# A hand-written TensorE order through the compressed, selected-key and window attention of a hybrid transformer block

## The chip, the cores and the metric

One core of one Trainium2 chip. The metric is the device time of one execution in microseconds (us), the median of three runs. In the rows, PE is TensorE (matmuls; PEld its weight loads), DVE is VectorE, ACT is ScalarE, POOL is GpSimd, SP is SyncE, which issues the DMAs.

## What is computed

One block over 512 tokens of width 1024: a mixer of three attentions with gates, a memory attention, a SwiGLU feed-forward network, a last norm. All is fp32. The part around the change, cut from the reference:

```python
o_a = _stick_breaking(q_a, k_a, v_a)                 # branch 0
o_b = _dsa_attention(...)                            # branch 1
o_c = _nsa_attention(...)                            # branch 2
g = sigmoid(p['g_merge'])                            # u @ w_in, 3 x 1024 columns
merged = g[0]*(o_a @ w_up[0]) + g[1]*(o_b @ w_up[1]) + g[2]*(o_c @ w_up[2])
h = h + merged @ w_out
# _dsa_attention, per block of 128 queries, 4 heads:
score = einsum('bqh,bqhk->bqk', wi, relu(qi . k_idx)); causal mask
sel = top_k(score, 128)                              # min(256, 512 // 4)
o_b = softmax over the selected keys (one k and v for all heads)
# _nsa_attention, per block of 128 queries, 4 heads:
o_c = gb[0]*softmax(q . kc) @ vc                     # 31 compressed keys
    + gb[1]*causal softmax(q . k_sel) @ v_sel        # all 8 blocks of 64 are selected
    + gb[2]*window softmax(q . k_win) @ v_win        # window 512: all causal keys
```

## The kernel before

**Number format.** Each fp32 operand of the large products is split into a high and a low part, and each product is three matmuls (`mm3`, L94 to L96: high by high, high by low, low by high). The weight tiles come by DMA from SP through rings: `load_fill` (two tiles; high part cast on ACT at L58, low part subtracted on POOL at L66) and `load_split` (three tiles; low part on DVE, L66).

**Stages.** Norm and projections; the stick-breaking attention (branch 0); then the part of the change; then memory attention, `w_out`, feed-forward network, last norm. The 512 queries go in tiles i = 0 to 3 of 128; query tile i sees (i + 1) x 128 keys.

**C attention** (branch 2, lines 618 to 624). For each tile three units: compressed keys (`cmp_attention`), selected blocks and window (`rows_attention`, once each). A `rows_attention` unit has for each of four heads two score matmuls (L292, L293) into one of the two banks of the pool `gm`, a fused subtraction and minimum on DVE that empties the bank (L578) and an exponential on ACT (L579). Then come a reciprocal, four scalings (L586 on ACT), and for each 128 keys `apply_v`: four transposes (L565), a copy out of PSUM (L58 or L60), and two value matmuls (a `pair`, L101) that add into the bank `av`. `pr`, which holds the probabilities, has two buffers; `pt`, the transposed copy, three.

**Selected-key attention B** (branch 1). Its keys are chosen by 16 rounds for each of tiles 1 to 3 (`topk_rounds`): DVE searches the eight largest scores of each row (L615) and replaces them (L616), over 256, 384 or 512 columns. 96 instructions in all. Then a mask (L631) and four `rows_attention` units with scalings and copies on DVE (lines 633 to 637).

**Gates and merges.** `fill_gate(j, f)` is one gate, 128 columns of branch j: 24 matmuls of 128x512 into one of the two banks of the pool `gf`, then a tanh on ACT. There are eight for each branch; three for branch 0 stand earlier in the program. `merge_up` multiplies a branch by `w_up` (eight steps of six matmuls), takes the product with the gate on DVE and adds the branches on POOL. In the program all of these stand behind both attentions (lines 639 to 646).

**What sets the order.** The kernel is written through a framework whose scheduler orders each engine's instructions when the program is built: among those that its own cost model holds ready, the one that is earliest in the program goes first. So gate matmuls, latest in the program, fill in where it holds attention work not to be ready, and the top-k rounds, later in the program than C, fill DVE in the same way. On the chip every engine then takes its instructions strictly in that order, each waiting until its inputs and its buffer are there.

```python
    for i in range(NT):
        o_ps = av_ps.tile([P, 2, P], F32, name="av")
        cmp_attention(i, o_ps, True, False)
        rows_attention(i, qc, ksel, vs["vsel"], causal_bias(i), gates[:, i, 1::3], o_ps, False, False)
        rows_attention(i, qc, kwin, vs["vwin"], causal_bias(i), gates[:, i, 2::3], o_ps, False, True)
        split(o_c[0][:, :, cc(i)], o_c[1][:, :, cc(i)], o_ps, scale=0.5)
    for r in range(16):
        for x in range(1, NT):
            topk_rounds(x, 1)
```

Of the kernel before, what the change touches and what calls it, by code (L numbers as in the profile page):

```python
# [7 lines left out]
F32 = mybir.dt.float32  # L8
# [18 lines left out]
def block_kernel(ctx: ExitStack, tc: tile.TileContext, A, out, dbg=None):  # L27
# [337 lines left out]
    def merge_gate(j, f, g, load, bank, cols=slice(0, S)):  # L365

        w = load((NK, P), [col_view(w_in, 2128 + j * D + f * P, P)])
        for k in range(NK):
            mm3(bank, [t[:, k, :] for t in w], [t[:, k, cols] for t in uT], k == 0, k == NK - 1)
        if j == 0 and f < early_g:  # L370
            nc.scalar.copy(g, bank)
        else:
            nc.scalar.activation(g, bank, AF.Tanh, scale=0.5)

    def fill_gate(j, f, n=S):
        g_t[j, f] = gp_.tile([P, S], F32, name="g", bufs=16)
        gp = gf_ps.tile([P, 512], F32, name="gf")
        merge_gate(j, f, g_t[j, f][:, :n], load_split if j == 1 and f % 2 else load_fill, gp[:, :n], slice(0, n))
# [11 lines left out]
    def merge_up(j, name, load, up_ps, n=S):  # L390
        for f in range(NK):
            if f % 4 == 0:
                w = load_up(j, f // 4, load)
            g, first = g_t[j, f][:, :n], g_t[0, f][:, :n]
            if j == 0 and f < early_g:
                with tc.issue_after(last_exp[0]):
                    nc.scalar.activation(g, g, AF.Tanh, scale=0.5)
            up = up_ps.tile([P, 512], F32, name=up_tag[up_ps is gf_ps])
            add_up(w, f, name, g, up[:, :n], slice(0, n))
            if j == 1:  # L400
                nc.vector.tensor_add(first, first, g)
                split(mg[0][:, f, :n], mg[1][:, f, :n], first, lo_eng=nc.gpsimd)
            elif j == 2:
                nc.gpsimd.tensor_add(first, first, g)

    for f in range(early_g):
        fill_gate(0, f)
# [153 lines left out]
    def apply_v(o_ps, v, src, first, last, k=P, eng=nc.scalar):  # L561

        tp = ps.tile([P, 4, P], F32, name="ps")
        for h in range(4):
            nc.tensor.transpose(tp[0:k, h, :], src[:, h, :], ident)  # L565
        pt = mq.tile([P, 4, P], F32, name="pt", bufs=3)
        copy(eng, pt[0:k], tp[0:k])
        pair(o_ps, [v, v], [pt[0:k, x::2, :] for x in range(2)], first, last)

    def rows_attention(i, q, k, v, bias, gate, o_ps, first, last, eng=nc.scalar):  # L570
        n = (i + 1) * P
        pr = mq.tile([P, 4, 512], F32, name="pr", bufs=2)
        nm = mq.tile([P, 4], F32, name="nm", bufs=2)
        den = mq.tile([P, 4], F32, name="den", bufs=2)
        for h in range(4):
            st = gm_ps.tile([P, 512], F32, name="gm")
            scores(st[:, :n], q[:, h, cc(i)], [t[:, 0:n] for t in k])
            nc.vector.tensor_tensor_reduce(pr[:, h, :n], st[:, :n], bias, -1.0, 3e38, ALU.add, ALU.min, nm[:, h:h + 1])  # L578
            nc.scalar.activation(pr[:, h, :n], pr[:, h, :n], AF.Exp, bias=nm[:, h:h + 1], scale=-1.0, accum_out=den[:, h:h + 1])  # L579
        sc = mq.tile([P, 4], F32, name="sc", bufs=2)  # L580
        nc.vector.reciprocal(sc, den)
        if gate is not None:
            nc.vector.tensor_mul(sc, sc, gate)
        for h in range(4):
            if eng is nc.scalar:
                nc.scalar.activation(pr[:, h, :n], pr[:, h, :n], AF.Copy, scale=sc[:, h:h + 1])  # L586
            else:
                nc.vector.tensor_scalar(pr[:, h, :n], pr[:, h, :n], sc[:, h:h + 1], None, op0=ALU.mult)
        for j in range(i + 1):
            apply_v(o_ps, v[:, j, :], pr[:, :, cc(j)], first and j == 0, last and j == i, eng=eng)  # L590

    def cmp_attention(i, o_ps, first, last):
        s = mq.tile([P, 4, 32], F32, name="cs")
        st = ps.tile([P, 4, P], F32, name="ps")
        for h in range(4):
            scores(st[:, h, 0:32], qc[:, h, cc(i)], kc)
        nc.vector.tensor_add(s, st[:, :, 0:32], cmpb[:, i, :].unsqueeze(1).to_broadcast([P, 4, 32]))
        m = mq.tile([P, 4], F32, name="nm", bufs=2)
        nc.vector.tensor_reduce(m, s, axis=AX.X, op=ALU.max)
        nc.vector.tensor_scalar(m, m, -1e20, None, op0=ALU.max)  # L600
        nc.vector.tensor_sub(s, s, m.unsqueeze(2).to_broadcast([P, 4, 32]))
        nc.scalar.activation(s, s, AF.Exp)
        den = mq.tile([P, 4], F32, name="den", bufs=2)
        nc.vector.tensor_reduce(den, s, axis=AX.X, op=ALU.add)
        nc.vector.tensor_scalar(den, den, 1e-30, None, op0=ALU.max)
        sc = mq.tile([P, 4], F32, name="sc", bufs=2)
        nc.vector.reciprocal(sc, den)
        nc.vector.tensor_mul(sc, sc, gates[:, i, 0::3])
        nc.vector.tensor_mul(s, s, sc.unsqueeze(2).to_broadcast([P, 4, 32]))
        apply_v(o_ps, vc, s, first, last, k=32)  # L610
# [8 lines left out]
    for i in range(NT):  # L619
        o_ps = av_ps.tile([P, 2, P], F32, name="av")  # L620
        cmp_attention(i, o_ps, True, False)
        rows_attention(i, qc, ksel, vs["vsel"], causal_bias(i), gates[:, i, 1::3], o_ps, False, False)
        rows_attention(i, qc, kwin, vs["vwin"], causal_bias(i), gates[:, i, 2::3], o_ps, False, True)
        split(o_c[0][:, :, cc(i)], o_c[1][:, :, cc(i)], o_ps, scale=0.5)
    dump("o_c", o_c[0].bitcast(F32))
    for r in range(16):
        for x in range(1, NT):
            topk_rounds(x, 1)


    for i in range(1, NT):  # L631
        nc.vector.tensor_scalar(score[i], score[i], -2e38, NEG, op0=ALU.is_gt, op1=ALU.mult)
    o_b = o_pair("b", op)
    for i in range(NT):
        o_ps = av_ps.tile([P, 2, P], F32, name="av")
        rows_attention(i, qb, kb, vs["vb"], score[i] if i else causal_bias(0), None, o_ps, True, True, nc.vector)
        split(o_b[0][:, :, cc(i)], o_b[1][:, :, cc(i)], o_ps, scale=0.5)
    dump("o_b", o_b[0].bitcast(F32))
    for f in range(early_g, NK):
        fill_gate(0, f)  # L640
    merge_up(0, "a", load_fill, gf_ps)
    for f in range(NK):
        fill_gate(2, f)
    merge_up(2, "c", load_split, gm_ps)
    for f in range(NK):
        fill_gate(1, f, S // 2)
# [38 lines left out]
    merge_up(1, "b", load_split, gm_ps, S // 2)  # L685
# [14 lines left out]
    def merge_rest(fh):  # L700

        g = []
        for f in range(4 * fh, 4 * fh + 4):
            g.append(md.tile([P, S // 2], F32, name="gh", bufs=4))
            bank = wo_ps.tile([P, 512], F32, name="wo")
            merge_gate(1, f, g[-1], load_split, bank[:, 0:S // 2], half1)
# [219 lines left out]
```

## Time and profile before

| | |
|---|---|
| median of three runs | 898.68 us (898.36 to 898.72) |
| the profiled execution, and its span | 898.28 us, 896.5 us |
| mean granted clock of PE | 0.994 of full speed |
| PE busy | 856.3 us, 96%, 5012 matmuls |
| DVE, ACT, POOL busy | 507.8 us (57%), 411.5 us (46%), 140.7 us (16%) |
| C and B attention with their fill of gates | about 191 to 300 us of the span |

The profile is one execution, on its own time axis from the span's start. A row of a timeline reads: start, duration, engine, line, operation, output <- inputs, shape; "x4" joins four equal ones; in brackets at the end stand the idle time ahead of the row and what ended it. Matmuls are pipelined, so the duration of one is longer than the step from one start to the next; steps are what adds up. A windows row gives each engine's busy time and instruction count in a stretch, the granted clock (PEclk; 1.00 is 2.4 GHz) and the DMA share.

### The profile page before, as it was taken

What the parts mean: (1) busy time and instruction counts of PE and PEld (TensorE: products, weight loads), DVE (VectorE), ACT (ScalarE), POOL (GpSimd) and SP (SyncE); (2) the same over time, 40 slices, a digit from 0 to 9 for tenths busy, and PEclk for the clock granted to TensorE, in tenths of its full rate; (3) what the DMA queues carried; (4) which work ended last, traced back from release to release, by engine and by line L of the source; (5) the groups of instructions that cost most, each with busy time, mean ns of one, the idle gap of its engine ahead of it and who ended that gap; (6) DMA issues with size and microseconds to landing.
All of it is one profiled execution on the core that took longest, in us unless ns stands there. A gap on an engine that the chain in (4) does not pass through costs nothing.

```text
span 896.5 us, 13084 instructions
## 1 busy us (share of the span) xinstructions
PE 856.3 (96%) x5012; PEld 731.7 (82%) x5012; DVE 507.8 (57%) x1155; ACT 411.5 (46%) x779; POOL 140.7 (16%) x116
## 2 busy tenths in 40 slices
PE   5999999899989999999989999999999999999995
PEld 5987899787757788978878979988888888888884
DVE  4456378799998305676677758643443334322226
ACT  6487545557774224544654545432322333211123
POOL 4021232302211347430232010000000000000002
PEclk9999999999999999999999999999999999999998
DMA  9340124510210334558446514642333332333312
GB/s 323 85 110 24 43 58 119 141 48 24 70 26 24 95 94 141 187 174 246 125 150 199 165 49 142 187 142 94 97 102 105 97 94 94 118 94 95 99 42 94
DMA packets 93710, 99.00 MB, mean 110 GB/s; under 512 B 4656, under 2 KB 81616, under 8 KB 93648
## 3 DMA queue, kind: packets, MB, share of 16 engines
q1 hardware_dynamic: 91568, 92.75, 34.0%
q10 hardware_dynamic: 2080, 5.42, 1.9%
q8 instruction: 39, 0.64, 0.3%
q14 instruction: 23, 0.19, 0.1%
HBM read 96.06 MB, written 2.10 MB: 109 GB/s over the span
## 4 chain that ended last, share of the span: by engine, by line
PE 85%; DVE 7%; ACT 4%; issue 2%; DMA 1%; POOL 0%; ACTq 0%; DVEq 0%; POOLq 0%
PE wo L95 9%; PE wo L96 9%; PE wo L94 9%; PE gf L94 6%; PE gf L95 6%; PE gf L96 6%; PE ff L94 4%; PE ff L95 4%; PE ff L96 4%; PE gm L94 3%; PE gm L95 3%; PE gm L96 3%; PE y L96 2%; PE y L94 2%; PE y L95 2%; PE av L101 2%
## 5 line engine op out<-in xcount | busy, mean ns | idle before, releaser
L58 ACT CAST whi<-raw 128x1024 fp32r<-128x1024 f32 (+1 forms) x167 | 174.8, 1048 | 292.4 <-PE y L96 78.9
L66 DVE TENSOR_TENSOR wlo<-raw,whi 128x1024 fp32r<-128x1024 f32 (+1 forms) x131 | 164.1, 1255 | 211.2 <-ACT whi L58 210.9
L66 POOL TENSOR_TENSOR wlo<-raw,whi 128x1024 fp32r<-128x1024 f32 x36 | 88.9, 2474 | 312.9 <-ACT whi L58 267.1
L95 PE MATMUL wo<-ut_lo,whi 128*128 128x256 f32 (+1 forms) x320 | 105.2, 329 | 0.0
L96 PE MATMUL wo<-ut_hi,wlo 128*128 128x256 f32 (+1 forms) x320 | 104.6, 327 | 0.0
L94 PE MATMUL wo<-ut_hi,whi 128*128 128x256 f32 (+1 forms) x320 | 104.4, 326 | 0.0
L96 PE MATMUL gf<-ut_hi,wlo 128*128 128x512 f32 (+1 forms) x192 | 69.8, 363 | 0.0
L94 PE MATMUL gf<-ut_hi,whi 128*128 128x512 f32 (+1 forms) x192 | 69.3, 361 | 0.0
L95 PE MATMUL gf<-ut_lo,whi 128*128 128x512 f32 (+1 forms) x192 | 69.3, 361 | 0.0
L94 PE MATMUL ff<-ut_hi,whi 128*128 128x512 f32 (+1 forms) x192 | 67.9, 354 | 0.0
L95 PE MATMUL ff<-ut_lo,whi 128*128 128x512 f32 (+1 forms) x192 | 67.9, 354 | 0.0
L96 PE MATMUL ff<-ut_hi,wlo 128*128 128x512 f32 (+1 forms) x192 | 67.9, 354 | 0.0
L95 PEld LDWEIGHTS wo<-ut_lo,whi 128*128 128x128 f32 x320 | 60.9, 190 | 6.2 <-issue 1.0
L94 PEld LDWEIGHTS wo<-ut_hi,whi 128*128 128x128 f32 x320 | 60.8, 190 | 5.8 <-issue 0.7
L96 PEld LDWEIGHTS wo<-ut_hi,wlo 128*128 128x128 f32 x320 | 60.8, 190 | 5.6 <-issue 0.4
L875 POOL TENSOR_TENSOR ut_hi<-ut_hi,ut_lo 128x512 f32<-128x512 f32 x4 | 5.0, 1276 | 367.0 <-ACT ut_hi L874 367.0
L94 PE MATMUL gm<-whi,ut_hi 128*128 128x256 f32 (+1 forms) x160 | 47.4, 296 | 0.0
L95 PE MATMUL gm<-wlo,ut_hi 128*128 128x256 f32 (+1 forms) x160 | 46.4, 290 | 0.0
L96 PE MATMUL gm<-whi,ut_lo 128*128 128x256 f32 (+1 forms) x160 | 46.3, 289 | 0.0
L96 PEld LDWEIGHTS gf<-ut_hi,wlo 128*128 128x128 f32 x192 | 36.2, 188 | 5.6 <-issue 1.2
L95 PEld LDWEIGHTS gf<-ut_lo,whi 128*128 128x128 f32 x192 | 36.2, 188 | 5.4 <-issue 0.8
L94 PEld LDWEIGHTS gf<-ut_hi,whi 128*128 128x128 f32 x192 | 36.2, 188 | 5.3 <-issue 0.8
(329 smaller groups left out, 2027.7 us busy)
## 6 DMA issues: line engine op xcount, KB each, us to landing
raw<-in_w_ffn_in_dram SPq DMA_DIRECT2D x56, 512.0 KB, 3.6
raw<-in_w_in_dram SPq DMA_DIRECT2D x46, 512.0 KB, 3.9
raw<-in_w_ffn_out_dram SPq DMA_DIRECT2D x22, 512.0 KB, 3.5
raw<-in_w_out_dram SPq DMA_DIRECT2D x16, 512.0 KB, 3.6
raw<-in_w_up_dram SPq DMA_DIRECT2D x8, 512.0 KB, 4.0
xt<-in_x_dram SPq DMA_DIRECT2D x4, 512.0 KB, 9.0
raw<-in_w_mem_kv_dram SPq DMA_DIRECT2D x4, 512.0 KB, 3.8
raw<-in_w_mem_q_dram SPq DMA_DIRECT2D x4, 512.0 KB, 3.8
```

Of the source, the lines that this page charges most:

```text
L58: nc.scalar.copy(dst, src)
L66: (lo_eng or nc.vector).tensor_sub(dst_lo, src, dst_hi.bitcast(F32))
L94: nc.tensor.matmul(dst, lh, rh, start=first, stop=False, skip_group_check=True)
L95: nc.tensor.matmul(dst, lh, rl, start=False, stop=False, skip_group_check=True)
L96: return nc.tensor.matmul(dst, ll, rh, start=False, stop=last, skip_group_check=True).ins
L101: nc.tensor.matmul(dst[64 * x:64 * x + 64], lhs[x], rhs[x], start=first, stop=last, skip_group_check=True)
L875: nc.gpsimd.tensor_mul(yo[:, n], yo[:, n], gain[:, n])
```

## The change

The same instructions are computed on the same engines; the order is changed. The order of PE within C, top-k and B is now the order in which the program text calls it (`tc.manual_schedule` with PE in it); the other engines are still ordered by the scheduler, with the new text as its input.

To write that order, the steps become generators. A `Rows` or `Compressed` unit yields after each head's scores and between its transposes and its value matmuls. Gates and merges become `filler`, one chain of jobs in the order of before (gates 3 to 7 of branch 0, merge of branch 0, gates of branch 2) that yields after every three gate matmuls, counted as 0.7 us, or six merge matmuls, counted as 1.4 us. `attend` walks the units: it takes the scores of a unit in turn with the transposes and values of the unit before, and after every step it draws gate or merge pieces from `filler`. How many comes from constants (`work`: the unit's own PE time; `busy`: time of its chain on other engines; factor 1.2). `pieces` asks for the weights of a job one job ahead. Between C and B 12 us of filler are drawn. What is left of the filler, the merge of branch 2 and the gates of branch 1 come after, ordered by the scheduler as before.

```diff
-    def fill_gate(j, f, n=S):
...
+    def gate_pieces(w, j, f, g, bank, cols=slice(0, S)):
+
         for k in range(NK):
             mm3(bank, [t[:, k, :] for t in w], [t[:, k, cols] for t in uT], k == 0, k == NK - 1)
+            yield 0.7 * (cols.stop - cols.start) / S
...
+    def pieces(jobs):
+
+        w = jobs[0][0]()
+        for i, (_, body) in enumerate(jobs):
+            ahead = jobs[i + 1][0]() if i + 1 < len(jobs) else None
+            yield from body(w)
+            w = ahead
...
+    fill_jobs = [gate_job(0, f) for f in range(early_g, NK)] + up_jobs(0, "a", load_fill, gf_ps) + [gate_job(2, f) for f in range(NK)]
+    filler = pieces(fill_jobs)
...
+    def fill_in(us):
+
+        owed[0] += us
+        while owed[0] > 0.3:
+            took = next(filler, None)
+            if took is None:
+                break
+            owed[0] -= took
...
+    class Rows:
...
+            n = (i + 1) / 4
+            self.work = (1.0 + n, 2.6 * (i + 1) * 0.45)
+            self.busy = (2.0 + 4.0 * n, 2.4 * n) if eng is nc.scalar else (1.6 + 3.6 * n, 2.8 * n)
...
+        def values(self, o_ps):
+            for j0 in range(0, self.i + 1, 2):
+                js = range(j0, min(j0 + 2, self.i + 1))
+                pts = [turn_rows(self.pr[:, :, cc(j)], P, self.eng) for j in js]
+                yield
+                for j, pt in zip(js, pts):
+                    apply_v(o_ps, self.v[:, j, :], pt, self.first and j == 0, self.last and j == self.i)
+                yield
...
+    class Compressed:
...
+            self.work, self.busy = (1.0, 1.4), (6.0, 0.8)
...
+    def attend(units, o, slack):
+
+        prev, o_ps = None, None
+        for u in units + [None]:
+            sc = u.scores() if u else iter(())
...
+                va = prev.values(o_ps)
+            free = slack * ((u.busy[0] if u else 0) + (prev.busy[1] if prev else 0)) - (u.work[0] if u else 0) - (prev.work[1] if prev else 0)
+            free = max(free, 1.5)
+            inner = min(1.0, free / 5)
+            next(sc, None)
+            left = 2
+            while left:
+                left = 0
+                for it in (sc, va):
+                    if next(it, it) is not it:
+                        left += 1
+                if left:
+                    fill_in(inner)
+                    free -= inner
+            fill_in(max(free, 0.0))
...
+    with tc.manual_schedule(engines={mybir.EngineType.PE}):
+        attend([u for i in range(NT) for u in (
+            Compressed(i),
+            Rows(i, qc, ksel, vs["vsel"], causal_bias(i), gates[:, i, 1::3], False, False),
+            Rows(i, qc, kwin, vs["vwin"], causal_bias(i), gates[:, i, 2::3], False, True))], o_c, 1.2)
+        dump("o_c", o_c[0].bitcast(F32))
+        for r in range(16):
+            for x in range(1, NT):
+                topk_rounds(x, 1)
...
+        fill_in(12.0)
+
+
+        attend([Rows(i, qb, kb, vs["vb"], score[i] if i else causal_bias(0), None, True, True, nc.vector)
+                for i in range(NT)], o_b, 1.2)
```

How that moves the instructions is shown at three places.

The first is PE where the projections end and C begins. In the order before (`ps<-cst,stk` at L253 are the transposes of the last rotary halves, `ps<-cst,rel` and the `ht` rows the end of the compression, `gf` a gate):

```order
L511 MATMUL ps<-cst,rel 128x32 x2
L292 MATMUL gm<-ksel_hi,qc 128x128
L293 MATMUL gm<-ksel_lo,qc 128x128
...
L94 MATMUL gf<-ut_hi,whi 128x512
L95 MATMUL gf<-ut_lo,whi 128x512
...
L519 MATMUL ps<-ht,w2t 128x32
L520 MATMUL ps<-w2t,ht 32x64
L253 MATMUL ps<-cst,stk 128x128 x4
...
L253 MATMUL ps<-cst,stk 128x128 x4
L292 MATMUL ps<-kc_hi,qc 128x32
```

and in the changed one:

```order
L532 MATMUL ps<-cst,rel 128x32 x2
L540 MATMUL ps<-ht,w2t 128x32
L541 MATMUL ps<-w2t,ht 32x64
L253 MATMUL ps<-cst,stk 128x128 x8
L292 MATMUL ps<-kc_hi,qc 128x32
L293 MATMUL ps<-kc_lo,qc 128x32
...
L94 MATMUL gf<-ut_hi,whi 128x512
L95 MATMUL gf<-ut_lo,whi 128x512
L96 MATMUL gf<-ut_hi,wlo 128x512
```

Four selected-key scores and ten gate matmuls that stood among the last rotary transposes now stand behind all eight of them and behind the first compressed scores; 27 gate matmuls follow these.

The second is PE in the unit of query tile 2, selected keys (scores of 128x384). Before (`cs` are the compressed probabilities, `vc` their values):

```order
L565 MATMUL ps<-cst,cs 32x128 x4
L292 MATMUL gm<-ksel_hi,qc 128x384
L293 MATMUL gm<-ksel_lo,qc 128x384
L292 MATMUL gm<-ksel_hi,qc 128x384
L293 MATMUL gm<-ksel_lo,qc 128x384
L565 MATMUL ps<-cst,pr 128x128 x2
L96 MATMUL gf<-ut_hi,wlo 128x512
L101 MATMUL av<-pt,vc 64x256 x2
```

and in the changed order:

```order
L292 MATMUL gm<-ksel_hi,qc 128x384
L293 MATMUL gm<-ksel_lo,qc 128x384
L292 MATMUL gm<-ksel_hi,qc 128x384
L293 MATMUL gm<-ksel_lo,qc 128x384
L599 MATMUL ps<-cst,cs 32x128 x4
L94 MATMUL gf<-ut_hi,whi 128x512
L95 MATMUL gf<-ut_lo,whi 128x512
L96 MATMUL gf<-ut_hi,wlo 128x512
L292 MATMUL gm<-ksel_hi,qc 128x384
L293 MATMUL gm<-ksel_lo,qc 128x384
L101 MATMUL av<-pt,vc 64x256 x2
```

Before, the third score pair comes some 35 rows later, among gates; now it comes three gate matmuls after the transposes, and the fourth three more after that.

The third is DVE ahead of the first subtraction of that unit. Before:

```order
L616 MATCH_REPLACE score_1248<-m_3235,score_1248 128x512
L597 TENSOR_TENSOR cs<-ps,cst 128x128
L616 MATCH_REPLACE score_1246<-m_3238,score_1246 128x256
L599 TENSOR_REDUCE nm<-cs 128x4
L578 ISA pr,nm<-gm,cst 128x384
L578 ISA nm 128x1
```

and in the changed order (the rounds are now L717 and L718, the subtraction L626):

```order
L717 MAX m_3611<-score_1247 128x8
L718 MATCH_REPLACE score_1246<-m_3608,score_1246 128x256
L718 MATCH_REPLACE score_1247<-m_3611,score_1247 128x384
L717 MAX m_3614<-score_1248 128x8
L717 MAX m_3617<-score_1246 128x8
L626 ISA pr,nm<-gm,cst 128x384
L626 ISA nm 128x1
```

Of the 96 top-k instructions 38 stand ahead of that subtraction before, 84 in the changed order. The order of the loads on SP is the same in both.

## Rows read from the trace of the kernel before

**Rows 1.** The page, its first section: busy time of each engine over the span

```profile
PE 856.3 (96%) x5012; PEld 731.7 (82%) x5012; DVE 507.8 (57%) x1155; ACT 411.5 (46%) x779; POOL 140.7 (16%) x116
```

**Rows 2.** Windows: length, busy PE, PEld, DVE, ACT, POOL, clock, DMA, GB/s

```profile
196.00:255.00 59.00, 58.68 (x346) 43.97 (x345) 55.93 (x223) 45.59 (x120) 9.57 (x4) 1.00 0.16 45
255.00:268.60 13.60, 10.17 (x65) 5.43 (x63) 13.46 (x46) 9.94 (x20) 2.37 (x1) 1.00 0.15 39
268.60:272.00 3.40, 3.29 (x12) 3.00 (x13) 2.79 (x14) 2.08 (x9) 0.00 (x0) 0.51 0.00 1
272.00:284.00 12.00, 10.73 (x61) 7.89 (x60) 10.89 (x40) 8.08 (x24) 2.37 (x1) 1.00 0.17 45
303.00:375.00 72.00, 71.91 (x405) 62.32 (x404) 23.27 (x31) 26.07 (x37) 42.09 (x20) 1.00 0.45 131
```

**Rows 3.** Waits of PE, 190 to 375 us: total, times, longest

```profile
PE gm L292 <- DVE nm L578: 2.9, 4, 1.5
PE av L101 <- ACT pt L58: 2.0, 3, 0.9
```

**Rows 4.** Timeline of PE, 266 to 269 us, the two waits ahead of half clock

```profile
266.58 0.65 PE L101 MATMUL av<-pt,vwin 128*64 128x256 f32 x4 [0.73 <-ACT pt L58]
...
268.71 0.48 PE L292 MATMUL gm<-kb_hi,qi 128*128 128x128 f32 x1 [1.48 <-DVE nm L578]
```

**Rows 5.** Timeline of PE, 241 to 245 us

```profile
241.70 1.63 PE L101 MATMUL av<-pt,vwin 128*64 128x256 f32 x12
243.26 0.28 PE L292 MATMUL ps<-kc_hi,qc 128*128 128x32 f32 x1
...
244.18 0.48 PE L96 MATMUL gf<-ut_hi,wlo 128*128 128x512 f32 x1
244.49 0.39 PE L94 MATMUL gf<-ut_hi,whi 128*128 128x512 f32 x1
244.72 0.40 PE L95 MATMUL gf<-ut_lo,whi 128*128 128x512 f32 x1
```

**Rows 6.** Timeline of PE, 191 to 196 us: the start of C

```profile
191.06 0.33 PE L292 MATMUL gm<-ksel_hi,qc 128*128 128x128 f32 x1
...
195.61 0.26 PE L292 MATMUL ps<-kc_hi,qc 128*128 128x32 f32 x1
```

**Rows 7.** Timeline of DVE, the last rotary half

```profile
194.38 0.41 DVE L66 TENSOR_TENSOR stk<-t,stk 128x256 fp32r<-128x256 f32 x1
```

**Rows 8.** Timeline of DVE, 202 to 206 us: a stretch of top-k rounds

```profile
202.30 0.08 DVE L616 MATCH_VALUE_LOAD score<-m,score 128x8 f32 x1
...
202.70 1.14 DVE L615 MAX8 m<-score 128x8 f32<-128x384 f32 x2
203.76 0.07 DVE L616 MATCH_VALUE_LOAD score<-m,score 128x8 f32 x1
...
204.28 0.08 DVE L616 MATCH_VALUE_LOAD score<-m,score 128x8 f32 x1
...
204.94 0.16 DVE L581 RECIPROCAL sc<-den 128x4 f32<-128x4 f32 x1
205.02 0.39 DVE L615 MAX8 m<-score 128x8 f32<-128x256 f32 x1
205.34 0.14 DVE L583 TENSOR_TENSOR sc<-sc,gates 128x4 f32<-128x4 f32 x1
```

**Rows 9.** Timeline of DVE, the first subtraction of 128x384

```profile
224.22 0.55 DVE L578 CUSTOM_DVE_ANT_0 pr<-gm,cst 128x384 f32<-128x384 f32 x1
```

**Rows 10.** Timeline of PE, 282 to 284 us: twelve transposes in a row

```profile
282.54 1.47 PE L565 MATMUL ps<-cst,pr 128*128 128x128 f32 x12
283.76 0.48 PE L96 MATMUL gm<-o_hi,wlo 128*128 128x512 f32 x1
```

**Rows 11.** Timeline of ACT, the scalings of one unit at 384 keys

```profile
230.90 2.13 ACT L586 ACTIVATE pr<-pr,sc 128x384 f32<-128x384 f32 x4
```

**Rows 12.** Timeline of PE, the transposes of the memory attention

```profile
374.73 1.04 PE L133 MATMUL ps<-cst,h 128*128 128x128 f32 x8
```

More of the change, by code (lines that the diff above doesn't have):

```diff
@@ L388, in add_up, with up_pieces @@
         nc.vector.scalar_tensor_tensor(g, g, 1.0, up, op0=ALU.add, op1=ALU.mult)
[L390 to L393, printed above, removed]
+    def up_pieces(w, j, fh, name, up_ps, n=S):
+        for f in range(4 * fh, 4 * fh + 4):
             g, first = g_t[j, f][:, :n], g_t[0, f][:, :n]
@@ L404, in merge_up, with gate_job, body, up_jobs @@
                 nc.gpsimd.tensor_add(first, first, g)
+            yield 1.4 * n / S
+    def gate_job(j, f, n=S):
+        load = load_split if j == 1 and f % 2 else load_fill
+        def body(w):
+            g_t[j, f] = gp_.tile([P, S], F32, name="g", bufs=16)
+            gp = gf_ps.tile([P, 512], F32, name="gf")
+            yield from gate_pieces(w, j, f, g_t[j, f][:, :n], gp[:, :n], slice(0, n))
+        return lambda: load_gate(j, f, load), body
+    def up_jobs(j, name, load, up_ps, n=S):
+        return [(lambda fh=fh: load_up(j, fh, load), lambda w, fh=fh: up_pieces(w, j, fh, name, up_ps, n)) for fh in range(2)]
+    def pieces(jobs):
[4 more added lines that the diff above has]
+            w = ahead
+    def finish(it):
+        for _ in it:
+            pass
     for f in range(early_g):
-        fill_gate(0, f)
+        finish(pieces([gate_job(0, f)]))
     a_st.close()
@@ L559, in block_kernel, with turn_rows @@
     mq = pool(mq_st, "mq")
-    def apply_v(o_ps, v, src, first, last, k=P, eng=nc.scalar):
+    fill_jobs = [gate_job(0, f) for f in range(early_g, NK)] + up_jobs(0, "a", load_fill, gf_ps) + [gate_job(2, f) for f in range(NK)]
+    filler = pieces(fill_jobs)
+    owed = [0.0]
+    def fill_in(us):
[5 more added lines that the diff above has]
+            owed[0] -= took
+    def turn_rows(src, k, eng):
         tp = ps.tile([P, 4, P], F32, name="ps")
@@ L567, in apply_v @@
         copy(eng, pt[0:k], tp[0:k])
+        return pt
+    def apply_v(o_ps, v, pt, first, last, k=P):
         pair(o_ps, [v, v], [pt[0:k, x::2, :] for x in range(2)], first, last)
[L570 to L590, printed above, removed]
@@ new lines, in attend @@
+    def attend(units, o, slack):
+        prev, o_ps = None, None
+        for u in units + [None]:
+            sc = u.scores() if u else iter(())
+            va = iter(())
+            if prev:
+                if prev.first:
+                    o_ps = av_ps.tile([P, 2, P], F32, name="av")
+                va = prev.values(o_ps)
[13 more added lines that the diff above has]
+            fill_in(max(free, 0.0))
+            if prev and prev.last:
+                split(o[0][:, :, cc(prev.i)], o[1][:, :, cc(prev.i)], o_ps, scale=0.5)
+            prev = u
@@ L618, in block_kernel @@
     o_c = o_pair("c", mq)
[L619 to L632, printed above, removed]
-    o_b = o_pair("b", op)
[L634 to L646, printed above, removed]
+    o_b = o_pair("b", op)
+    with tc.manual_schedule(engines={mybir.EngineType.PE}):
[7 more added lines that the diff above has]
+                topk_rounds(x, 1)
+        for i in range(1, NT):
+            nc.vector.tensor_scalar(score[i], score[i], -2e38, NEG, op0=ALU.is_gt, op1=ALU.mult)
+        fill_in(12.0)
+        attend([Rows(i, qb, kb, vs["vb"], score[i] if i else causal_bias(0), None, True, True, nc.vector)
+                for i in range(NT)], o_b, 1.2)
+        dump("o_b", o_b[0].bitcast(F32))
+    finish(filler)
+    for jobs in (up_jobs(2, "c", load_split, gm_ps), [gate_job(1, f, S // 2) for f in range(NK)]):
+        finish(pieces(jobs))
     mq_st.close()
@@ L683, in block_kernel @@
     kv_st.close()
-    merge_up(1, "b", load_split, gm_ps, S // 2)
+    finish(pieces(up_jobs(1, "b", load_split, gm_ps, S // 2)))
     first1 = [h[2 + f // 4][:, f % 4 * 256:f % 4 * 256 + 256] for f in range(NK)]
@@ L705, in merge_rest @@
             bank = wo_ps.tile([P, 512], F32, name="wo")
[L706 removed]
+            finish(gate_pieces(load_gate(1, f, load_split), 1, f, g[-1], bank[:, 0:S // 2], half1))
         w = load_up(1, fh, load_split)
```

80 lines of the change are left out of this document (56 added, 24 removed).

## The prediction, made before the changed kernel had run

> **What bounds the kernel now.** I began with the page: TensorE (PE) is busy 96% of the span [rows 1], so the time is, to first order, PE's list of matmuls. The change deletes none of them; it can win only what PE loses between them and lose only by new gaps. So I went to the windows of the attention, where the order changes [rows 2]: from 196 to 255 us PE is busy 58.68 of 59.00, and VectorE (DVE) 55.93 of 59.00. The reader should see two engines full at once. From 255 to 284 PE loses 3.43, 0.11 and 1.27 us, and for 3.40 us its granted clock is 0.51, that is 1.2 GHz instead of 2.4. The waits view names the releasers [rows 3]: score matmuls behind a subtraction on DVE that frees their bank, value matmuls behind a copy on ScalarE (ACT). The timeline shows the fall of the clock behind waits of 0.73 and 1.48 us [rows 4]. From 303 to 375 us PE is busy 71.91 of 72.00 with the gates that are left over, so a microsecond lost or won before arrives there whole.
>
> Why is PE full for 59 us beside a full DVE? Because in the old order whatever is not ready is replaced by gate matmuls, and DVE's top-k rounds (L615, L616) are put where they delay few scores. Both orders are fixed when the program is built. So the question is not PE's order alone but how it meets DVE's, and the change moves DVE's order too.
>
> **The change, part by part.** All sums stand against the profiled execution, 898.28 us; the median of the runs, 898.68, is 0.4 above it. About 0.2% (1.8 us) is what a measurement of this kernel can tell from no change.
>
> *The idle that goes.* If the new order filled every gap from 196 to 284 us, it would save 0.32, 3.43, 0.11 and 1.27 us of idle [rows 2] and half of the 3.40 us at half clock, 1.7: together 6.8 us. I credit all of it, since the new order has gates mixed in at these units too, where the old one had few left; from 5, if some of the old waits come back, to 6.8.
>
> *Fewer changes of kind.* From the first selected-key score to the memory transposes the order changes between gate, score, transpose and value matmuls 185 times before and 128 times after. A steady 512-column gate matmul steps 0.23 us; the one just behind a block of another kind steps 0.31 (244.18 to 244.49 against 244.49 to 244.72) [rows 5]. Not every change costs that (to and from scores it costs nothing), so of 57 fewer I take 1 us, between 0 and 2.
>
> *The entry.* Before, while DVE finishes the last rotary halves, PE runs four score matmuls and ten gate matmuls among the last transposes, from 191.06 to 195.61 [rows 6]. In the new order all eight transposes come first, and nothing may pass them. The last four need what DVE writes at 194.38, in 0.41 us [rows 7], so PE reaches the compressed scores at about 195.3 us, hardly earlier than the 195.61 of before, but with ten gate matmuls (10 x 0.23) and four scores (0.46, at the price of the compressed ones [rows 5]) still to do: 2.8 less 0.3, **+2.5 us**, between 2 and 3.
>
> *DVE's queue.* This is the large term. The order view shows how many of the 96 top-k instructions stand ahead of the first subtraction of query tile 2, selected keys (128x384): 38 before, 84 after. The 46 that move ahead are 8 searches of each width and 7, 8 and 7 replacements at 256, 384 and 512. Start to start, with the short value load in it, the rows give 0.32 for a search at 256, 1.06 for those at 384 and 512 together, and 0.40, 0.52 and 0.66 for the replacements [rows 8]. 8 x (0.32 + 1.06) + 7 x 0.40 + 8 x 0.52 + 7 x 0.66 = 22.6 us. Nothing else of weight changes sides. DVE did that first subtraction at 224.22 [rows 9] with next to no idle since 196, so it now comes to it at about 224.2 + 22.6 = 246.8.
>
> When is PE there? Ahead of that unit the new order puts, from 195.3 on, 114 gate matmuls of 0.233, 24 compressed-score matmuls of 0.115 (three tiles' eight), 32 other score matmuls at the same price, 32 transposes of 0.10 (twelve in 1.22 us) and 8 value pairs of 0.52 (three in 1.56 us) [rows 5, 10]: 26.6 + 2.8 + 3.7 + 3.2 + 4.2 = 40.5 us, so 235.8 if it never waits. Two score pairs, four transposes and three gate matmuls later, at 237.6, stands the third score pair. There are two banks, so it needs the first subtraction done: 246.8 + 0.55 = 247.4. PE stands 9.8 us late, wherever the wait is paid, there or at earlier units. The gates behind it can't pass. In the old order the same wait was covered by gates; the cover is gone because the written order hands out a fixed number of pieces for each step and the waiting step blocks the rest. **+9.8 us**, between 7.5 (some of the rounds overlap better than in these rows) and 11 (DVE itself idles, waiting for PE, earlier).
>
> Afterwards DVE is late no more: it has 12 of the 96 top-k instructions left, about 6 us, and its subtractions, while PE has 193 gate and merge matmuls (45 us) before the attention's last value matmul, beside its scores.
>
> *ACT's chain.* From tile 2 on each unit's transposes stand behind the four scalings of that unit (2.13 us at 384 columns [rows 11]), and value matmuls behind a copy. PE has 12 gate matmuls (2.8 us) ahead of the scalings of the selected keys, but six or fewer elsewhere. The nearest rows are the three waits on that copy, 2.0 us [rows 3]. I take **+2**, from 0 to 6.
>
> The gate and merge work itself has its weights in time: the loads keep their order on SP, each gate lasts 24 x 0.233 = 5.6 us, and from 303 us on the same ring fed gates back to back [rows 2]. The later gates for branch 1, their loads and POOL's part stand as before.
>
> **Sum.** 898.28 - 6.8 - 1 + 2.5 + 9.8 + 2 = 904.8; I say **905 us**, slower by 0.7%. All low ends together give about 898, all high ends 913.
>
> **The clock.** The row shows a fall to 1.2 GHz of 3.40 us behind waits of 0.4 to 1.5 us [rows 2, 4], price 1.7. The new order has about 10 us of waits between 203 and 248. Half speed costs little while PE waits for DVE anyway, so I put nothing in the sum.
> The Trainium skill, page "TensorE: Matmul & The Clock Gate", section "A second HAM failure mode: psum-queue depth-cycling", says that short idles between matmul groups can make the clock swing between its two levels, at a cost to throughput. By that rule the sum would be higher, by the first rival's 4 us; the trace agrees for one place of several with such waits.
>
> **The rivals.**
> (1) *The clock falls again and again* in the DVE-bound part: for it speaks the one fall behind waits of this size; against it, that the other short waits of the trace had none. Two or three falls whose matmuls lie outside the waits, 1.7 each, less what hides: +4, 909 us. Chance 0.17.
> (2) *Faster: the lag does not form.* The place is the third score pair of tile 2; the point is DVE's arrival. The sum without lag is 898.28 - 6.8 - 1 + 2.5 + 2 = 895.0. It stays under 898.3 if DVE comes less than 3.3 us after PE, so if the 46 moved instructions took under 16.1 us instead of 22.6. For it: DVE's busy share counts overlapped ends, and it idled 3.07 of 59 us. Against it: the steps are start to start, and the queue was full. About 895, chance 0.09.
> The Trainium skill, page "Perfetto Trace Analysis", section "Optimization Strategy", advises to interleave stretches that load different engines; by that rule this change should gain. The trace holds against it that the stretch was interleaved already, with PE and DVE both full.
> (3) *About even:* lag at its low end, no ACT waits, 898 to 900.4 us. Chance 0.10. That the change does not do what it says is not open: the order view shows the new sequence on PE.
>
> **How the numbers follow.** The forecast's own case, 901 to 908 us, has 0.64, rival (1) 0.17, even 0.10, faster 0.09. The range of 8 in 10 leaves out the faster case and the top of the first rival: 898 to 912. Faster by over 0.2%: 0.09; within: 0.10; slower: 0.81.
>
> **What would show it.** Right: in the profile after, PE waits on score matmuls, transposes and value matmuls between 203 and 248 us that sum to some 10 us; DVE busy over 19 of 20 us up to about 250 and slack after; the first subtraction at 128x384 near 247; the transposes of the memory attention, which stand behind the last gate, near 381 instead of 374.73 [rows 12], with everything behind them only shifted. A PE gap near 191 to 195 shows the entry. Wrong: if that subtraction comes near 237 (no lag: faster), if idle appears behind 260 us of more than 5 us (ACT's chain or the weights' ring), or if the granted clock is low in several places.

## The result, and the profile after

The changed kernel takes **919.15 us** (median of four, 918.21 to 921.86) against 898.7: ratio 1.0225, 95% interval 1.0206 to 1.0245. The direction was forecast; the size was not (905, range 898 to 912). The profiled execution is the slowest of the four, 921.86 us with a span of 920.0, 23.5 above that of before.

The page of the changed kernel, first section (answers to [rows 1]):

```profile
PE 869.1 (94%) x5012; PEld 738.5 (80%) x5012; DVE 515.1 (56%) x1155; ACT 412.6 (45%) x779; POOL 138.8 (15%) x116
```

PE is 12.8 us busier with the same 5012 matmuls. The windows of the changed kernel (columns as in [rows 2]): the entry in two pieces, C in three, and the whole stretch up to the transposes of the memory attention.

```profile
191.00:193.20 2.20, 0.26 (x3) 0.17 (x3) 2.20 (x8) 1.90 (x4) 0.00 (x0) 1.00 0.06 10
193.20:203.30 10.10, 10.00 (x33) 8.20 (x34) 8.27 (x30) 1.99 (x5) 0.00 (x0) 0.51 0.37 102
203.30:255.00 51.70, 44.24 (x223) 32.24 (x221) 47.60 (x168) 25.16 (x68) 9.57 (x4) 0.96 0.14 41
255.00:268.60 13.60, 11.02 (x50) 7.36 (x48) 12.58 (x39) 9.51 (x23) 2.40 (x1) 0.87 0.15 40
268.60:284.00 15.40, 14.72 (x86) 10.68 (x83) 10.45 (x27) 6.67 (x16) 2.38 (x1) 1.00 0.13 36
...
190.96:396.78 205.82, 190.03 (x1016) 145.57 (x1016) 130.04 (x384) 98.80 (x220) 56.72 (x27) 0.96 0.25 72
```

The last of these in the kernel before, up to its own memory transposes [rows 12]:

```profile
190.96:374.73 183.77, 178.55 (x1014) 139.84 (x1014) 122.58 (x384) 97.70 (x220) 58.52 (x27) 0.99 0.28 79
```

The stretch is 22.05 us longer: 15.79 us of idle instead of 5.22, and 11.5 us more of busy time for the same work. Half clock explains part of the latter: (1 - clock) x busy is 4.9, 1.8 and 1.4 us in the rows 193.20, 203.30 and 255.00, against 1.6 before, so 6.5 more. The other 5 us lie in the transposes. Summed from the timeline of PE (each matmul's start to the next one's, less the idle time between them), the 144 transposes of the stretch take 21.2 us, 1.6 of them by half clock, against 14.0 before; all the other matmuls together take, half clock taken off, no longer than before. A wait that lies inside such steps is in none of PE's idle rows. Waits of PE in the changed kernel, 185 to 400 us (answers to [rows 3]):

```profile
PE ps L599 <- ACT pr L636: 5.8, 9, 1.4
PE av L101 <- ACT pt L58: 3.4, 5, 1.1
PE gm L292 <- DVE nm L626: 2.8, 2, 1.8
PE ps L540 <- ACT whi L58: 2.0, 1, 2.0
```

and the same view of the weight loads (PEld), which show a wait for each matmul, also where the matmul records run into each other:

```profile
PEld ps L599 <- ACT pr L636: 10.5, 23, 1.6
PEld av L101 <- ACT pt L58: 7.5, 14, 1.4
...
PEld gm L292 <- DVE nm L626: 3.8, 3, 2.1
```

In the kernel before these three were:

```profile
PEld av L101 <- ACT pt L58: 6.6, 14, 1.1
PEld gm L292 <- DVE nm L578: 5.6, 8, 1.9
...
PEld ps L565 <- ACT pr L586: 1.7, 4, 0.5
```

So the wait that grew most is that of the **transposes for ACT's scalings**, 10.5 us for 1.7; the wait for subtractions, which I had made the largest term, is no longer than before. The timeline of PE shows its form, and the entry:

```profile
193.21 0.51 PE L540 MATMUL ps<-ht,w2t 128*128 128x32 f32 x2 [1.95 <-ACT whi L58]
...
237.71 1.96 PE L599 MATMUL ps<-cst,pr 128*128 128x128 f32 x8 [1.38 <-ACT pr L636]
239.43 0.36 PE L292 MATMUL gm<-kwin_hi,qc 128*128 128x256 f32 x1
...
253.88 0.34 PE L292 MATMUL gm<-ksel_hi,qc 128*128 128x384 f32 x1
...
256.89 0.44 PE L292 MATMUL gm<-ksel_hi,qc 128*128 128x384 f32 x1 [1.01 <-DVE nm L626]
...
396.78 1.47 PE L133 MATMUL ps<-cst,h 128*128 128x128 f32 x12
```

Eight transposes take 1.72 us (237.71 to 239.43) where twelve took 1.22 [rows 10]. ACT's timeline beside them:

```profile
237.17 1.69 ACT L636 ACTIVATE pr<-pr,sc 128x256 f32<-128x256 f32 x4
```

Four scalings, one for each head, 0.4 us apart; the first four transposes step at that pace, one behind each. And the scalings waited themselves, for DVE: their factor is a reciprocal (L631) times the gate (L633). The waits of ACT for that product, after and, in the second row, before:

```profile
ACT pr L636 <- DVE sc L633: 6.1, 6, 2.0
...
ACT pr L586 <- DVE sc L583: 0.4, 1, 0.4
```

In the unit above the product stands behind a subtraction of the next unit, for whose scores DVE first waits 0.50 us; in four others of the eight `rows_attention` units of C, top-k instructions stand in between.

```profile
235.47 0.16 DVE L631 RECIPROCAL sc<-den 128x4 f32<-128x4 f32 x1
236.13 0.42 DVE L626 CUSTOM_DVE_ANT_0 pr<-gm,cst 128x256 f32<-128x256 f32 x1 [0.50 <-PE gm L293]
...
236.48 0.38 DVE L633 TENSOR_TENSOR sc<-sc,gates 128x4 f32<-128x4 f32 x1
```

DVE's timeline also has the subtraction that I had put at 246.8:

```profile
256.30 0.53 DVE L626 CUSTOM_DVE_ANT_0 pr<-gm,cst 128x384 f32<-128x384 f32 x1
```

### The profile page after: what moved, and what is told of

The parts are those of the page before. It is cut to its first block, busy times and chain, and to the rows that moved or that the text cites. A ratio compares the mean times of both kernels' runs of the same rounds, so it can differ in the third digit from the quotient of the medians.

```text
span 920.0 us, 13071 instructions
## 1 busy us (share of the span) xinstructions
PE 869.1 (94%) x5012; PEld 738.5 (80%) x5012; DVE 515.1 (56%) x1155; ACT 412.6 (45%) x779; POOL 138.8 (15%) x116
## 4 chain that ended last, share of the span: by engine, by line
PE 78%; DVE 12%; ACT 5%; issue 2%; DMA 1%; POOL 0%; ACTq 0%; DVEq 0%; POOLq 0%
PE wo L95 8%; PE wo L96 8%; PE wo L94 8%; PE gf L94 5%; PE gf L95 5%; PE gf L96 5%; PE ff L96 4%; PE ff L94 4%; PE ff L95 4%; PE gm L94 2%; PE gm L95 2%; PE gm L96 2%; PE y L96 2%; PE y L94 2%; PE y L95 2%
## 5 line engine op out<-in xcount | busy, mean ns | idle before, releaser
L66 POOL TENSOR_TENSOR wlo<-raw,whi 128x1024 fp32r<-128x1024 f32 x36 | 87.0, 2422 | 346.9 <-ACT whi L58 301.2
L94 PE MATMUL gf<-ut_hi,whi 128*128 128x512 f32 (+1 forms) x192 | 73.5, 383 | 0.0
L94 PEld LDWEIGHTS gf<-ut_hi,whi 128*128 128x128 f32 x192 | 37.3, 194 | 10.5 <-issue 5.5
```

What stands on the lines that cost most here:

```text
L66: (lo_eng or nc.vector).tensor_sub(dst_lo, src, dst_hi.bitcast(F32))
L94: nc.tensor.matmul(dst, lh, rh, start=first, stop=False, skip_group_check=True)
```

## The experiments

The theories: **D**, the top-k instructions that moved ahead on DVE (my large term). **E**, the entry: 1.95 us of idle and 10.1 us at half clock behind it. **A**, the chains through ACT: transposes and value matmuls stand too few matmuls behind the scaling or copy that they wait for. **G**, a lock-step in which what is gained at one place is waited for at the next. Ratios are to the kernel before, run beside each.

### e1: the rounds held back (D)

```diff
...
         for r in range(16):
+            held = 0 if r < 1 else 2 if r < 3 else 5 if r < 6 else 8 if r < 11 else 11
             for x in range(1, NT):
-                topk_rounds(x, 1)
+                with tc.issue_after(c_units[held].mark) if held else ExitStack():
+                    topk_rounds(x, 1)
```

(`c_units` are C's twelve units in order, `mark` is a unit's last subtraction; the rounds stand behind it on DVE.)

> The changed kernel, with the top-k rounds held back on DVE: round 1 and 2 behind the last subtraction of tile 0, rounds 3 to 5 behind that of tile 1, 6 to 10 behind tile 2, 11 to 15 behind tile 3, so that 36 of the 96 top-k instructions stand ahead of the first subtraction of 128x384 instead of 84 (38 in the kernel before). PE's order is that of the change. Theory D (the moved top-k instructions are the main loss): 9 to 10 us come back, about 909 us. Theory E (the idle at 191 us and the half clock behind it) and theory A (the transposes stand too close behind the scalings on ACT): under 3 us come back, 916 us or more.

920.01 us, 1.022 (1.0196 to 1.0244): nothing came back. Its waits of PE:

```profile
PE av L101 <- ACT pt L58: 7.8, 9, 1.6
PE ps L599 <- ACT pr L636: 3.8, 10, 1.2
```

The wait for subtractions fell from 2.8 to 0.5 us, that for copies rose from 3.4 to 7.8.

### e2: the entry filled (E)

```diff
     o_b = o_pair("b", op)
+    fill_in(2.8)
     with tc.manual_schedule(engines={mybir.EngineType.PE}):
```

> The changed kernel, with 2.8 us of the filler (12 gate matmuls) drawn ahead of the hand-ordered block, so that the scheduler may put them among the last rotary transposes, as the kernel before has ten. Theory E: no idle at 191 us, no half clock from 193 to 203, so 1.95 idle and about 5 us of clock come back: about 912 us. Theory D: DVE is behind by the same 46 instructions wherever PE starts, so PE waits for it later what it gained here: under 3 us come back, 916 or more.

921.62 us, 1.024 (1.0215 to 1.0265). The idle at 191 us is gone, and with it the fall of the clock there; but the window up to the memory transposes is no shorter:

```profile
190.90:398.06 207.16, 194.72 (x1029) 147.74 (x1028) 130.53 (x389) 100.17 (x221) 58.57 (x27) 0.94 0.24 71
```

The clock falls later instead (0.94 over the stretch, 0.96 in the change). Its longest stretch at half speed comes behind a wait for a subtraction on DVE, which is theory D's, and one of 0.55 us for a copy; the later ones come among waits for scalings.

```profile
206.80 0.33 PE L292 MATMUL gm<-ksel_hi,qc 128*128 128x128 f32 x1 [1.18 <-DVE nm L626]
...
208.00:221.00 13.00, 11.77 (x37) 8.32 (x34) 10.42 (x41) 5.97 (x21) 2.37 (x1) 0.50 0.14 42
```

Neither D nor E alone is worth anything.

### e3 and e4: where the hand-written order stops costing

e3 holds the order for B alone, e4 nowhere:

```diff
-    with tc.manual_schedule(engines={mybir.EngineType.PE}):
+    with ExitStack():
         attend([u for i in range(NT) for u in (
```

(e3 opens the hand-ordered block again ahead of B.)

> The new text, but the hand-written order of PE holds for the selected-key attention alone; the scheduler orders C. All three theories put the loss into C (the waits on scalings, copies and subtractions before 310 us): then within 4 us of the kernel before, 896 to 903 us. If the loss were B's or came from the rewritten text: 910 us or more.

898.74 us, 0.999 (0.9979 to 1.0002).

> The new text with no hand-ordered block at all: the scheduler orders PE, with gates and merges now standing between the attention's steps in the program, no longer behind them. If the loss lies in PE's fixed order: 895 to 902 us. If it lies in the rewritten text (gates earlier in the program go ahead of attention work that is ready, and DVE's rounds fill in as in the changed kernel): 908 us or more.

898.91 us, 0.9992 (0.998 to 1.0004). The whole loss is C's fixed order on PE; B's costs nothing, nor does the new text.

### e5: more filler in C

```diff
-            Rows(i, qc, kwin, vs["vwin"], causal_bias(i), gates[:, i, 2::3], False, True))], o_c, 1.2)
+            Rows(i, qc, kwin, vs["vwin"], causal_bias(i), gates[:, i, 2::3], False, True))], o_c, 1.6)
```

> The changed kernel with the factor of C raised from 1.2 to 1.6, so that about 30 us more of gates and merges stand between C's steps, most of them between a unit's last score and its transposes. Theory A (each hand-placed transpose and value matmul stands too few matmuls behind the ACT step that it waits for): the waits on the scalings (5.8 us, and some 4 hidden between the transposes) shrink, 909 to 913 us. Theory G (the waits are one lock-step between engines that all take their list in order, so what is gained at one place is waited for at the next; e1 and e2 gained nothing): 916 to 921 us. With the filler spent earlier, B may wait more in either case.

917.74 us, 1.0193 (1.0176 to 1.021). The scalings' wait falls to 1.2 us, but B, whose cover is spent, waits 2.7 us for its own, on DVE.

### e6: no top-k at all

The loop of 16 rounds is deleted; the kernel then leaves out the choice of keys of branch 1.

> The changed kernel with the 96 top-k instructions left out: the computation then lacks the choice of keys of branch 1, all else stands. Theory D in its strongest form (DVE's load is what makes PE wait in C): DVE has some 45 us less to do in C, and the time falls to 905 us or less. Theory A (ACT's chains behind PE's fixed order): the waits of transposes and value matmuls stay, 913 us or more.

915.48 us, 1.0162 (1.0147 to 1.0177). DVE is busy 83.3 us instead of 130.0 in the stretch, and still:

```profile
PE av L101 <- ACT pt L58: 6.7, 10, 1.1
PE ps L599 <- ACT pr L636: 2.8, 8, 1.2
PE ps L540 <- ACT whi L58: 2.1, 1, 2.1
```

D in its strong form falls here: the top-k load on DVE is not what makes this kernel slow, while the other two stand. The scalings still wait 5.6 us for DVE's product.

### e7 and e9: combinations that spend all the filler

Both have e1's and e2's edits and add the merge of branch 2 and the gates of branch 1 to the filler; e7 has factor 1.6, e9 1.2 and `fill_in(1.4)` between transposes and value matmuls.

> Four edits together on the changed kernel: the rounds held back (as in e1), 2.8 us of filler ahead of the block (as in e2), factor 1.6 for C, and the merge of branch 2 and the gates of branch 1 added to the filler behind C, so that B keeps its cover. If the three causes each hide behind the others: with all three gone 900 us or less. If the fixed order costs of itself (theory G): 908 us or more.

917.33 us, 1.0183 (1.0168 to 1.0198).

> As e7, but with the factor left at 1.2 and 1.4 us more filler drawn just between each group of transposes and its value matmuls. Theory A, the copy's part (7.8 us of waits of value matmuls on the copy in e1): those waits go below 2 us, and the time to 908 to 912 us. If the wait only moves on to the next unit's scalings: 916 us or more.

915.95 us, 1.0167 (1.0152 to 1.0182). In e9 the copies' wait is gone from the list, while the scalings' is 4.0 us. With the filler used up, B waits 5.5 (e7) and 4.2 us (e9) for scalings, and the memory transposes, which gates used to cover, wait 3.8 and 3.3 us for DVE.

### e10 and e13: the filler placed otherwise (A)

e10 draws half of it at a unit's end:

```diff
-            inner = min(1.0, free / 5)
+            inner = min(1.0, free / 10)
```

> The changed kernel with half of each unit's filler drawn at its end, ahead of the next unit's first score and so ahead of its own transposes, where the change spreads nearly all of it between the steps (free / 10 in place of free / 5). The amount is the same. Theory A: the scalings' waits shrink by half, 5 us seen and hidden together, and the scores' and copies' grow by some of it: 913 to 917 us. Theory G: 918 to 921.

919.35 us, 1.0232 (1.021 to 1.0254): scalings 5.8 to 1.9 us, copies 3.4 to 6.5. e13 covers both:

```diff
-            left = 2
-            while left:
...
+            for it in (sc, va):
+                while next(it, it) is not it:
+                    fill_in(inner)
+                    free -= inner
...
+            fill_in(gap[0])
             for j0 in range(0, self.i + 1, 2):
...
                 yield
+                fill_in(gap[0])
                 for j, pt in zip(js, pts):
```

(`gap` is 1.4; the compressed unit has it ahead of its value matmuls too; factor 0.9. So repair A has three parts: a unit's scores all ahead, filler ahead of the transposes and of the value matmuls, and a smaller factor. They were not tried apart.)

> The changed kernel, with C's filler put elsewhere: all four scores of a unit come ahead of the transposes of the unit before, 1.4 us of filler is drawn ahead of a unit's first transposes and 1.4 us between each group of transposes and its value matmuls, and the factor of C is 0.9 to pay for it. Top-k rounds and the entry stay as in the change. Theory A: the waits of transposes on the scalings (5.8 us seen, some 5 hidden where the four transposes step at the pace of the four scalings) and of value matmuls on the copy (3.4) fall below a third; waits of scores on the subtraction grow by some 2 us; 908 to 912 us. Theory G (the wait moves to the next step in the lock-step): 915 us or more.

914.48 us, 1.0175 (1.0154 to 1.0197). The scalings' wait is gone from PE and PEld, and now the subtractions are what PE waits for:

```profile
PE gm L292 <- DVE nm L626: 7.2, 8, 2.0
PE av L101 <- ACT pt L58: 2.9, 3, 1.5
PE ps L540 <- ACT whi L58: 1.9, 1, 1.9
```

That is theory D's lag, showing only once A is out of its way. Of the ranges set ahead of the runs, e5, e7 and e10 came out in theory G's, e9 and e13 within 0.6 us below its lower end.

### e11, e14, e15, e16: A, D and E together and in pairs

e11 is e13 with e1's and e2's edits; e14 is A and D, e15 A and E, e16 D and E.

> e13 with the rounds held back on DVE (e1) and the entry filled (e2) as well. If A is the bottleneck that hid the gain of those two, they now count: 3 to 7 us below e13, 902 to 907 us. If they still gain nothing: within 2 us of e13.

899.15 us, 1.0003 (0.9992 to 1.0013). Its waits of PEld have no row of transposes behind scalings any more:

```profile
PEld av L101 <- ACT pt L58: 3.9, 5, 2.3
PEld gm L292 <- DVE nm L626: 3.6, 6, 1.2
```

and its window is at full clock. Beside it stands that of the kernel before; both start behind the last `rel` matmul, so that they hold the same matmuls:

```profile
191.96:375.03 183.07, 178.41 (x1014) 138.01 (x1013) 129.51 (x384) 99.21 (x220) 55.94 (x27) 1.00 0.28 78
...
191.06:374.73 183.67, 178.45 (x1014) 139.78 (x1013) 122.47 (x384) 97.60 (x220) 58.52 (x27) 0.99 0.28 79
```

Here G falls as a cost of the fixed order as such: with the three causes repaired, an order of PE fixed by hand costs nothing. Its weaker sense, that a gain at one place is waited for at the next, is what the single repairs showed.

> e13's placement of the filler and the rounds held back (A and D), without the filled entry. e13 alone waits 7.2 us for subtractions, the lag of DVE that the prediction had put at 9.8. If D counts as soon as A is out of its way: 7 to 9 us below e13's 914.5, 905 to 908 us. If all of e11's further 15 us hang on the entry: 913 us or more.

908.62 us, 1.0095 (1.0074 to 1.0115).

> e13's placement and the filled entry (A and E), rounds as in the change. E takes away 1.9 us of idle and some 5 us of half clock. If E adds to A: 907 to 909 us. If PE, started earlier, only meets the same late DVE: 912 us or more, with the waits for subtractions grown by what the entry gave.

905.89 us, 1.0067 (1.0046 to 1.0088).

> D and E together with the filler placed as in the change (no A). If D and E are enough: 905 us or less. If the chains through ACT keep PE back until the transposes are moved: 912 us or more.

911.85 us, 1.0132 (1.0109 to 1.0155); its PEld rows for the two chains through ACT are about those of the changed kernel (10.5 and 7.5 us):

```profile
PEld ps L599 <- ACT pr L636: 9.7, 24, 1.7
PEld av L101 <- ACT pt L58: 9.6, 15, 1.3
```

| repaired | ratio to before | in us of 899 |
|---|---|---|
| nothing (the change) | 1.0225 | +20 |
| D / E / A | 1.022 / 1.024 / 1.0175 | +20 / +22 / +16 |
| D and E / A and D / A and E | 1.0132 / 1.0095 / 1.0067 | +12 / +9 / +6 |
| all three | 1.0003 | 0 |

Alone, D gives 0, E -1 and A 4 to 5 us (each is known to some 2 us); as the last of three they give 6 (D), 8 (E) and 12 (A). These overlap and are no shares of the 20. I read it so: the three are late chains side by side, and PE leaves with the latest. That is argued, not shown, and the clock has a part in it: by the rows, (1 - clock) x busy over the stretch is about 8 us in the change, 12 in e2, and nothing in e16 and e11.

### e12, e17, e18: an order below the kernel before

e12 and e17 are e4 with the rounds held; e17's stages are:

```diff
+            held = 2 if r < 2 else 5 if r < 6 else 8 if r < 11 else 11
```

(e12: round 0 behind the first rows unit, 1 and 2 behind tile 0.)

> e4 (the new text, PE ordered by the scheduler, 898.9 us) with the top-k rounds held back as in e1 and the first of them behind the first unit of tile 0. In e4 PE still waits 2.5 us for subtractions that stand behind top-k instructions, 1.4 of them at 203 us with 3 us of half clock behind it. If those waits go: 895 to 897 us. If the last rounds then end too late for B: 900 us or more.

897.66 us, 0.999 (0.9979 to 1.0002), not clear of the kernel before.

> e12 (scheduler's order, rounds held) with the rounds held one step longer: rounds 0 and 1 behind tile 0, 2 to 5 behind tile 1. In e12 the waits between 204 and 246 us are 2.5 us in sum. If they go: 895 to 897 us; if DVE then falls behind for B: 898 or more.

897.47 us, **0.9971** (0.9958 to 0.9983): below both kernels. PE waits 1.3 us for subtractions in place of 2.5 in e4, and the clock does not fall:

```profile
190.50:372.61 182.11, 179.97 (x1016) 138.39 (x1015) 128.66 (x384) 97.92 (x220) 56.70 (x27) 1.00 0.29 80
```

e18 holds the rounds in the same way in the kernel before.

> The kernel before, with nothing changed but the top-k rounds held on DVE as in e17 (0 and 1 behind tile 0's last subtraction, 2 to 5 behind tile 1's, 6 to 10 behind tile 2's, 11 to 15 behind tile 3's). If e17's gain comes from DVE's order alone: 896 to 898 us, as e17. If it needs the new text, in which gates stand between the attention's steps: 898.5 us or more, since the kernel before spends its gates early and lacks them at the waits between 255 and 284 us.

902.57 us, 1.0027 (1.0013 to 1.0041). One wait tells why:

```profile
275.05 0.47 PE L292 MATMUL gm<-kb_hi,qi 128*128 128x128 f32 x1 [6.32 <-DVE nm L580]
```

The old text puts B's first scores early; DVE still has held rounds to do, and PE has nothing in its order to put in their place. As far as these runs show, e17's gain of 0.3% needs both: the gates between the steps, as the change writes them, and the rounds spread.

## Why the prediction was wrong, point by point

**ACT's chain, +2 (0 to 6): the step that failed.** With D and E repaired, it costs 12 us (e16 against e11). I priced it by three waits of 2.0 us for copies [rows 3], and looked for waits of the scalings only where PE's own rows showed them, which was nowhere. What stood between was counted nearly right: in the trace, two score pairs or eight compressed scores and 3 to 12 gate matmuls, where the prediction has 12 and "six or fewer elsewhere". It was not set against the chain that has to run meanwhile: a subtraction, an exponential, on DVE a reciprocal and the product with the gate, each behind what else DVE has in its queue, and the scalings. In tile 1, selected keys, the last score pair starts at 232.60 us. The product comes at 236.48, the first scaling at 237.17, the first transpose at 237.71. PE has nine gate matmuls and two score pairs to do, is through at 236.33 and waits 1.38 us.

```profile
232.60 0.41 PE L292 MATMUL gm<-ksel_hi,qc 128*128 128x256 f32 x1
```

The chain is long in the scheduler's order too: in e4 the scalings wait 5.6 us for DVE's product, yet PE has no wait for scalings in its rows, for there other work stands in its list meanwhile.

**The entry, +2.5 (2 to 3): mis-sized.** PE reached the compressed scores at 195.94 us (forecast 195.3), after 1.95 us of idle. What I left out is the clock: from 193.20 to 203.30 us PE is busy 10.00 us at 0.51, so 4.9 us more. The term measures 8 us as a last repair (e14 against e11), the clock included.

**DVE's queue, +9.8 (7.5 to 11): the mechanism is there, the sum was wrong.** As a last repair it measures 6 us (e15 against e11), and e13 shows its waits. In the changed kernel itself PE waits no longer for subtractions than before. "Wherever the wait is paid" failed: DVE had slack (busy 47.60 of 51.70 us where I had forecast over 19 of 20), for it waited for PE's scores, as PE waited for ACT. The first subtraction at 384 came at 256.30, not 246.8, because PE issued its scores at 253.88, 18 us later than the 235.8 of my count.

**The idle that goes, -6.8, and changes of kind, -1: the first hardly there.** With all three causes repaired (e11) PE's idle is 183.07 - 178.41 = 4.66 us against 5.22, and the clock stays up, yet the stretch is only 0.6 us shorter. What the clock gave back went into the steps of the 600 gate and merge matmuls: summed from the timeline as above, 124.9 us in e11 at full clock, against 123.4 before with half clock taken off. In e16, also at full clock, they take 122.2 us, so there the credit of 1 us shows; why e11 loses it, the runs don't settle.

**The clock, 0, and rival (1), +4.** It fell in three stretches, 6.5 us more half clock than before. I had set it aside because "half speed costs little while PE waits for DVE anyway"; between the waits PE had work all the time (busy 44.24 of 51.70 us in the stretch from 203.30).

**The sum.** Five terms added up as if each lay alone on the path gave the right side and a third of the size. The side is no luck, since all three costs are real; but the largest of them was not what the changed kernel paid. Errors did not cancel: the large credit was not earned, the clock stood at nothing, and two of the three costs were three to six times too small. (The low ends of the terms add up to 899, not 898; nothing hangs on it.)

**The rivals.** (1) had its mechanism, three falls of the clock, but not its price, 909. (2) fell: no lag shows, yet nothing is faster. (3) fell with the time. Two of the signs of being wrong came: the clock was low in several places, and behind 260 us PE was idle for more than 5 us.

```profile
260.00:396.78 136.78, 131.50 (x743) 102.30 (x742) 66.94 (x166) 66.31 (x135) 47.15 (x23) 0.99 0.29 84
```

That the memory transposes would only shift what is behind them holds: from them to the span's end it takes 523.2 us, 521.8 before.

The Trainium skill, page "Perfetto Trace Analysis", section "Identifying the Most-Contended Engine", says that matmul busy share is a poor measure of how near TensorE is to its limit, and names the share of peak FLOPs and the weight loads' busy share instead. The trace agrees in that busy time is no measure of work: from 191 us to the memory transposes PE's rises from 178.55 to 190.03 us for the same matmuls. The loads' share says no more than PE's here, as both fall by five points: PEld from 139.84 of 183.77 us, 76%, to 145.57 of 205.82, 71%; PE from 97 to 92%.

## What to carry to other kernels

An order fixed on one engine must leave, between each producer's start and its consumer, as much work as the whole chain on the other engines takes with their queues; here an even spread of filler covered no link of it fully. Look at the waits of the weight loads as well as of the matmuls: here short waits in a row, head by head, were in no idle row of PE. And where one repair after another gains little, try them together before any is thrown away: here they gave 0, -1 and 4 to 5 us singly and 20 together.

## What the runs showed that I had not expected

The clock does not follow the idle total. e2 has 12.4 us of idle in its window and a clock of 0.94 (its row stands under e2); e16, which is e2 with the rounds held, has 11.5 us and 1.00:

```profile
190.90:386.19 195.29, 183.81 (x1022) 140.40 (x1021) 127.53 (x386) 99.04 (x221) 58.64 (x27) 1.00 0.26 74
```

Each is one execution: over the whole span the clocks of e16's four lie between 0.988 and 0.994, and the profiled one is among the best. By the edits, only the held rounds separate the two kernels, and e16 has no wait for a subtraction in PE's rows, where e2's long fall stands behind one. Which waits make the clock fall was not tried.

The Trainium skill, page "TensorE: Matmul & The Clock Gate", section "A second HAM failure mode: psum-queue depth-cycling", says that short idles between groups of matmuls can make the clock swing between its levels. e2's trace agrees, e16's does not.
